# Neighbourhood attention in an encoder kernel: the value product as out[query, dim] in full tiles, the softmax division at the eviction, and q's low part padded with zeros

## The chip, the cores and the metric

The kernel runs on one core of one Trainium2 chip. The metric is device microseconds of that core from the start to the end of one execution, as the median of several runs. Five engines work side by side, each through its own list of instructions in order: PE (TensorE, matrix products), DVE (VectorE), ACT (ScalarE), POOL (GpSimd) and SP, which here only issues DMAs. [...]

## What is computed

One layer of a hybrid encoder over 16 meta tokens and 1024 tokens (a grid of 16 rows by 64 columns), width 1024. One input projection feeds three groups of heads, which are gated, concatenated and go through one output projection. The diff touches the first group, neighbourhood attention with 8 heads of 64, and in passing the second, gated linear attention (GLA) with 4 heads.

```python
s_loc = einsum('bhcd,bhrckd->bhcrk', qr, kw) * scale + bias      # a window of 8 rows x 16 columns of keys
s = concatenate([s_loc.reshape(B, H, GRID_W, wr * WIN_C), s_meta], axis=-1)
p = softmax(s, axis=-1)
o = einsum(p_loc, vw) + einsum(p_meta, vm_h)                     # then o * silu(g)
...
b = cumsum(g, axis=-2)                                           # GLA: within chunks of 64
```

## The kernel before

The program is built by a scheduler: Python generators emit instructions in an interleaved order, and the tile framework then orders each engine's list by its own timeline model, puts in the semaphores, and hands out the buffers of a tile's tag in rotation.

The work is staged. First comes the input projection (`proj_steps`, tile `pj`) interleaved with the RWKV branch, up to about 997 us. Then comes the stage that the change touches: for each pair of heads p = 0..3 the generator `na_mix(p)` is stepped by the loop at L1402, and at each step it is fed with five projection products of the next pair (`feed.pull`, tile `pj`), with one or two steps of GLA (`gla(h)`) and, for p = 3, with six products of the output projection (`out_pass`, tile `ops`). The output projection ends the program.

Float32 accuracy is kept by splitting: a tensor x is held as a rounded part and a remainder, both of type float32r (`whi`/`wlo`, `hhi`/`hlo`, `oh`/`ol`). For the scores, `na_k` stores per head e a tile `K[:, e]` whose one half of the partitions holds K and whose other half holds K's remainder; `na_q` stores q in `qA[:, e]` in both halves of the partitions and q's remainder in `qL`, where head e fills its own 64 partitions.

`na_mix(p)` goes over 16 items n: two halves of the query rows (hf), four column blocks (cb) and the two heads e of the pair, e innermost. One item is 128 queries (8 rows x 16 columns) against 288 to 416 keys:

- `score(n)` (L1194): two products into `sps`, q's high part (L1207, 128 rows) and its remainder (L1208, 64 rows). DVE adds the bias and takes the maximum into `sc` (L1211), ACT takes the exponent with the sum (L1216), DVE the reciprocal `rc` (L1218), and POOL multiplies `sc` by it and by 0.5 in place (L1219). `sc` has three buffers, `sps` one.
- `turn(n)` (L1223): three or four transposes of `sc` into `tps`, copied by ACT and DVE to `pT` (L1234).
- `value(n)` (L1241): for odd n, the products of both heads of the pair, `ops[half[e]]` with the values `VC` (or `VE` for the 17th row, 32 keys) as the stationary operand and `pT` moving. They write the transposed result out[dim, query] into tile `o_ps`, head 0 in partitions 0 to 63 and head 1 in 64 to 127. ACT copies it to `oT` (L1257). After the fourth column block POOL multiplies by the gate `gh` (L1259), and a DMA stores it (L1260).

The items overlap: at one step `score(n)`, `turn(n-1)` and `value(n-2)` are emitted.

In GLA (`gla(h)`, L1059) the head starts with a chain: `lps`, exponent and logarithm on ACT, a running sum over 17 chunks of 64 on DVE (three scans, L1080 to L1084, with the mask `smask`), two more exponents, the products `Q` and `MN`, then `aps`.

Of the kernel before, what the change touches and what calls it, by code (L numbers as in the profile page):

```python
# [12 lines left out]
ONB = 1  # L13
PM = 1
YM = 2
# [60 lines left out]
def emit(ctx, tc, a, out):  # L76
# [327 lines left out]
    def na_q(p, w):  # L404
        def ev_q(ps, n0, n1):
            third = (2 * p + n0 // 512) % 3 == 2
            pool = na if third else nst["pool"]
            qa = pool.tile([128, 2, 512], F32R, name="qA", bufs=1 if third else 2)
            ql = pool.tile([128, 512], F32R, name="qL", bufs=1 if third else 2)
            nst[p, "q", n0 // 512] = qa, ql  # L410
            blocked = lambda t: t.rearrange("p (b r c) -> p b r c", r=8, c=16)
            pv = ps.rearrange("p (r b c) -> p b r c", b=4, c=16)
            for e in range(2):
                S.copy(blocked(qa[half[e], e]), pv[half[e]])
            for e in range(2):
                V.tensor_tensor(out=blocked(ql[half[e]]), in0=pv[half[e]], in1=blocked(qa[half[e], e].bitcast(F32)), op=ALU.subtract)
                V.tensor_copy(qa[half[1 - e], e], qa[half[e], e].bitcast(F32))

        yield from proj_steps(w, GRID, ev_q)
# [629 lines left out]
    gl = gx.enter_context(tc.tile_pool(name="gl", bufs=1, side="right"))  # L1049
    smask = gl.tile([128, LP], BF16, name="smask2")  # L1050
    G.memset(smask, 1.0)
# [7 lines left out]
    def gla(h):  # L1059
# [9 lines left out]
        for (n0, n1) in FULL:  # L1069
# [9 lines left out]
        V.tensor_tensor(out=GB[:, PAD:], in0=MN[:, PAD:], in1=LG[:, PAD:], op=ALU.subtract)  # L1079
        V.tensor_tensor_scan(out=GB[0:64], data0=smask[0:64], data1=GB[0:64], initial=0.0, op0=ALU.mult, op1=ALU.add)  # L1080
        V.tensor_tensor_scan(out=GB[64:128, 0:C], data0=smask[64:128, 0:C], data1=GB[64:128, 0:C], initial=0.0,
                             op0=ALU.mult, op1=ALU.add)
        gr = GB[64:128, C:][:, ::-1]
        V.tensor_tensor_scan(out=gr, data0=smask[64:128, 0:T], data1=gr, initial=0.0, op0=ALU.mult, op1=ALU.add)  # L1084
        E1 = LG
# [41 lines left out]
        for n0 in range(0, NCH, 4):  # L1127
            m = min(4, NCH - n0)
            kps = pm.tile([64, 4, 128], F32, name="kps", tag="gt", bufs=2)
            for j in range(m):  # L1130
                PE.transpose(out=kps[:, j, :], in_=KD[:, (n0 + j) * C:(n0 + j + 1) * C], identity=ident)
            kdT = gl.tile([64, 4, 128], F32, name="kdT")
            S.copy(kdT[:, 0:m, :], kps[:, 0:m, :])
# [23 lines left out]
        for t0 in (0, 4):  # L1157
# [7 lines left out]
            ss = gl.tile([128, 4], F32, name="gs", bufs=2)  # L1165
            On = gl.tile([128, 4, 128], F32, name="On", bufs=ONB)
            for t in range(4):
# [15 lines left out]

    BT, SB, PTB = 3, 3, 2
    NE = G if 1 else V
    PTM = 1

    def na_mix(p):
        K, VC, VE = nst[p, "k"], nst[p, "v"], nst[p, "ve"]
        ohs = {}  # L1190
        order = [(hf, cb, e) for hf in range(2) for cb in range(4) for e in range(2)]
        us, bias = {}, {}

        def score(n):  # L1194
# [12 lines left out]
            PE.matmul(sv, lhsT=qa[:, e, cs], rhs=kv, start=True, stop=False)  # L1207
            PE.matmul(sv, lhsT=ql[es, cs], rhs=kv[es], start=False, stop=True)  # L1208
            sc = na.tile([128, 416], F32, name="sc", bufs=SB)
# [8 lines left out]
            V.reciprocal(rc, sm)  # L1218
            NE.tensor_scalar(out=sc[:, 0:m], in0=sc[:, 0:m], scalar1=rc, scalar2=0.5, op0=ALU.mult, op1=ALU.mult)  # L1219
            blocks = [(b, w, VC[0:w, cb, j, es] if j < 4 else VE[:, cb - 1, es]) for j, b, w in win_blocks(hf, cb)]  # L1220
            us[n] = sc, blocks

        def turn(n):  # L1223
            sc, blocks = us[n]
            tps = pm.tile([128, 4, 128], F32, name="tps", tag="t")
# [10 lines left out]
            else:  # L1236
                for j, (b, m, _) in enumerate(blocks):
                    (S.copy if j % 2 else V.tensor_copy)(pT[0:m, j, :], tps[0:m, j, :])
            us[n] = pT, blocks

        def value(n):  # L1241
            hf, cb, e = order[n]
            if not e:
                return
            pair = us.pop(n - 1), us.pop(n)
            ops = pm.tile([128, 128], F32, name="o_ps", tag="o")
            nb = len(pair[0][1])
            for j in range(nb):
                for e, (pT, blocks) in enumerate(pair):
                    _, m, vv = blocks[j]  # L1250
                    PE.matmul(ops[half[e]], lhsT=vv, rhs=pT[0:m, j, :], start=(j == 0), stop=(j == nb - 1))
            if hf not in ohs:
                gh = na.tile([128, 512], F32, name="gh")
                nc.sync.dma_start(out=gh, in_=nag[p][:, 512 * hf:512 * hf + 512])
                ohs[hf] = na.tile([128, 512], F32, name="oT"), gh
            oT, gh = ohs[hf]
            S.copy(oT.rearrange("p (r c) -> p r c", c=64)[:, :, 16 * cb:16 * cb + 16], ops.rearrange("p (r c) -> p r c", c=16))  # L1257
            if cb == 3:
                G.tensor_tensor(out=gh, in0=gh, in1=oT, op=ALU.mult)  # L1259
                nc.sync.dma_start(out=oscr[p][:, 512 * hf:512 * hf + 512], in_=gh)  # L1260

        TL, VL = 1, 2
        for n in range(16 + VL):
# [6 lines left out]
            if 0 <= n - VL < 16:  # L1270
                value(n - VL)
                if YM >= 3:
                    yield

# [282 lines left out]
```

## Time and profile before

| | us |
|---|---|
| median of three timed runs | 1490.52 (1487.98 to 1501.66) |
| the profiled execution | 1485.04 |
| its span, first to last instruction | 1482.8 |
| TensorE busy in the span | 1375.4 (93%) |
| DVE, ACT, POOL busy in the span | 886.2, 611.5, 665.7 |
| mean granted TensorE clock | 0.959 of full speed |

A matmul shows as a weight load (PEld) and a product (PE). A row of the timeline gives the start, how long it lasted, the engine, the line, out<-in by tile names, the array's tile shape (rows*columns of the stationary operand), the moving shape and how many followed each other. All products have the line of a helper (L93, transposes L96), so they are told apart by tiles. Products are pipelined: what one takes of the engine is the step from its start to the next start, and its recorded duration overlaps the next one's.

### The profile page before, as it was taken

To read this page: it belongs to the slowest core of one execution; us is meant where nothing else is said; L and a number is where in the kernel's file an instruction comes from. 1 tells how busy PE (TensorE), PEld (TensorE's weight loads), DVE (VectorE), ACT (ScalarE), POOL (GpSimd) and SP (SyncE) were. 2 spreads that over 40 slices of the span, in tenths; PEclk is the share of its full clock that TensorE was granted. 3 is DMA by queue.
4 is the path that set the end of the run, shared out by engine and by line. 5 is a ranking of instruction groups with operands and counts; after the bars stand their busy time and mean duration, and the time that the engine had idled before them with its cause. 6 is when DMAs were issued, how large, how long until landed. Compare 5 with 4: busy or idle time off the path is not lost. (4 is left out here: it accounts for less than half of the span.)

```text
span 1482.8 us, 36124 instructions
## 1 busy us (share of the span) xinstructions
PE 1375.4 (93%) x14656; PEld 1132.4 (76%) x14656; DVE 886.2 (60%) x1936; ACT 611.5 (41%) x1368; POOL 665.7 (45%) x775
## 2 busy tenths in 40 slices
PE   5888988999899999999999999998999989899997
PEld 4877777877788788788888888776677767667786
DVE  7425465676856565746656564546757577775554
ACT  5324243334443443434334332435465554644333
POOL 6435364464646664657656563223323132321223
PEclk9999898999989999999999999999999999899999
DMA  7655533433433444334333433155353423731432
GB/s 205 162 134 134 133 95 86 123 91 71 117 95 88 113 89 121 86 91 113 87 106 80 100 99 78 44 115 134 84 120 87 112 73 96 240 111 55 132 93 93
DMA packets 184806, 158.88 MB, mean 107 GB/s; under 512 B 19152, under 2 KB 168048, under 8 KB 184640
## 3 DMA queue, kind: packets, MB, share of 16 engines
q1 hardware_dynamic: 119616, 117.12, 26.6%
q0 software_dynamic: 63264, 35.20, 13.2%
q10 hardware_dynamic: 1760, 4.26, 0.8%
q8 instruction: 115, 1.88, 0.5%
q14 instruction: 51, 0.42, 0.1%
HBM read 123.81 MB, written 32.72 MB: 106 GB/s over the span
## 5 line engine op out<-in xcount | busy, mean ns | idle before, releaser
L93 PE MATMUL pj<-hhi,whi 128*128 128x348 f32 (+10 forms) x1088 | 378.9, 349 | 12.4 <-DVE zt L263 8.7
L93 PE MATMUL pj<-hlo,whi 128*128 128x348 f32 (+10 forms) x1088 | 377.0, 347 | 0.0
L93 PE MATMUL pj<-hhi,wlo 128*128 128x348 f32 (+8 forms) x1064 | 368.6, 347 | 1.7 <-POOL wlo L166 1.7
L93 PEld LDWEIGHTS pj<-hhi,whi 128*128 128x128 f32 (+1 forms) x1088 | 212.1, 195 | 28.2 <-issue 11.9
L93 PEld LDWEIGHTS pj<-hlo,whi 128*128 128x128 f32 (+1 forms) x1088 | 212.0, 195 | 12.9 <-issue 2.6
L93 PEld LDWEIGHTS pj<-hhi,wlo 128*128 128x128 f32 x1064 | 208.9, 196 | 14.4 <-issue 2.6
L166 POOL TENSOR_TENSOR wlo<-wraw,whi 128x512 fp32r<-128x512 f32 x94 | 125.6, 1337 | 144.6 <-DMA whi<-in_w_in_dram 53.6
L162 POOL DMA_DIRECT2D whi<-in_w_in_dram x94 | 74.7, 795 | 114.7 <-PE pj L93 101.3
L1219 POOL TENSOR_SCALAR sc<-sc,rc 128x288 f32<-128x288 f32 (+3 forms) x64 | 45.4, 710 | 163.9 <-DVE rc L1218 136.8
L845 POOL TENSOR_TENSOR dS<-SV,dec 64x128 f32<-64x128 f32 x128 | 59.1, 462 | 73.7 <-DVE SV L861 68.3
L699 POOL TENSOR_TENSOR BK<-BK,dec 64x1024 f32<-64x1024 f32 (+1 forms) x40 | 68.4, 1710 | 49.1 <-PE g L93 45.6
L791 ACT CAST XA<-ta 128x512 f16<-128x512 f32 (+1 forms) x92 | 49.9, 542 | 90.5 <-PE ta L93 87.3
L785 DVE TENSOR_TENSOR Fc<-fps,im 128x512 f16<-128x512 f32 (+1 forms) x92 | 58.5, 636 | 47.7 <-PE fps L93 43.6
L93 PE MATMUL ops<-hhi,oh 128*128 128x512 f32 x256 | 86.8, 403 | 0.0
L93 PE MATMUL g<-XR,BK 64*128 64x128 f32 (+1 forms) x544 | 67.6, 296 | 5.5 <-DVE GR L687 5.5
L93 PEld LDWEIGHTS g<-XR,BK 64*128 64x128 f32 x544 | 53.9, 192 | 16.5 <-issue 12.3
L1211 DVE CUSTOM_DVE_ANT_0 sc<-sps,bt 128x288 f32<-128x288 f32 (+3 forms) x64 | 33.3, 520 | 44.8 <-PE sps L93 30.4
L1328 DVE TENSOR_TENSOR yv<-ops,yv 128x512 f32<-128x512 f32 x48 | 33.0, 690 | 41.5 <-PE ops L93 41.3
L93 PEld LDWEIGHTS ops<-hhi,oh 128*128 128x128 f32 x256 | 48.6, 191 | 11.9 <-issue 1.0
L861 DVE TENSOR_TENSOR SV<-c,dS 64x128 f32<-64x128 f32 x128 | 36.7, 286 | 35.0 <-PE c L93 32.6
L257 ACT ACTIVATE zt<-pj,cols 128x347 f32<-128x347 f32 (+1 forms) x42 | 23.0, 549 | 82.5 <-PE pj L93 74.0
L93 PEld LDWEIGHTS <-Nh 64*64 64x64 f16 x1600 | 43.4, 111 | 15.0 <-issue 12.8
(302 smaller groups left out, 3048.7 us busy)
## 6 DMA issues: line engine op xcount, KB each, us to landing
whi<-in_w_in_dram POOLq DMA_DIRECT2D x94, 256.0 KB, 4.0
wraw<-in_w_in_dram SPq DMA_DIRECT2D x94, 256.0 KB
lr<-rwl POOLq DMA_DIRECT2D x32, 256.0 KB, 3.5
rwz<-zt SPq DMA_DIRECT2D x12, 544.0 KB
orr<-oscr SPq DMA_DIRECT2D x96, 64.0 KB
wr<-in_w_out_dram SPq DMA_DIRECT2D x12, 512.0 KB
glz<-zt SPq DMA_DIRECT2D x8, 544.0 KB
k<-rwz SPq DMA_DIRECT2D x32, 128.0 KB
```

The source lines that it names most:

```text
L93: return place(nc.tensor.matmul(*args, **kw))
L162: G.dma_start(out=hi, in_=w_v[:, q:q + 4, c0:c0 + 128])
L166: G.tensor_tensor(out=lo, in0=raw, in1=hi.bitcast(F32), op=ALU.subtract)
L257: S.activation(zt[:, PAD + n0:PAD + n1], ps[:, n0 - lo:n1 - lo], AF.Copy, scale=c1)
L699: G.tensor_tensor(out=bk, in0=bk, in1=dec[es, :, :, None, None].broadcast_to([64, 2, ns, 2, C]), op=ALU.mult)
L785: V.tensor_tensor(out=Fc, in0=fps, in1=mskt(l), op=ALU.mult)
L791: S.copy(A, aps)
L845: G.tensor_tensor(out=dS[es], in0=cur[es, :, e, :], in1=dcur[es, :, None].broadcast_to([64, 2, C]), op=ALU.mult)
L861: V.tensor_tensor(out=nx[es, :, e, :], in0=cps[es, 2], in1=dS[es], op=ALU.add)
L1211: V.tensor_tensor_reduce(out=sc[:, 0:m], in0=sps[:, 0:m], in1=bias[e][:, 0:m], scale=1.0, scalar=-3.0e38, op0=ALU.add, op1=ALU.max, accum_ ...
L1219: NE.tensor_scalar(out=sc[:, 0:m], in0=sc[:, 0:m], scalar1=rc, scalar2=0.5, op0=ALU.mult, op1=ALU.mult)
L1328: V.tensor_tensor(out=o, in0=ps, in1=o, op=ALU.add)
```

## The change

The value product is turned round. For each head e its own products are issued, `pT` as the stationary operand (128 queries) and the values moving (64 columns), into `o_ps[:, e]` as out[query, dim]; both heads of a pair share one PSUM tile. Since the queries are now on partitions, the division by the sum of exponents becomes the `scale` of the eviction on ACT (`AF.Copy` with `rc`), and the scaling on POOL goes. When a half's four column blocks are done, `close` transposes the four tiles [query, e and dim] into one PSUM tile `oT` (tag of `tps`, one buffer), DVE multiplies by 0.5 and the gate, and the DMA stores it.

q's remainder `qL` becomes two full tiles, one a head, with zeros in the other half of the partitions (a POOL memset each), so that both score products use 128 rows.

`sc` has two buffers instead of three, `smask` covers nine chunks instead of 17 (and the running sums are made in five scans instead of three), and `kdT` and `On` of GLA share a buffer.

```diff
-            ql = pool.tile([128, 512], F32R, name="qL", bufs=1 if third else 2)
+            ql = pool.tile([128, 2, 512], F32R, name="qL", bufs=1 if third else 2)
...
             for e in range(2):
-                V.tensor_tensor(out=blocked(ql[half[e]]), in0=pv[half[e]], in1=blocked(qa[half[e], e].bitcast(F32)), op=ALU.subtract)
+                G.memset(ql[half[1 - e], e].bitcast(F32), 0.0)
+                V.tensor_tensor(out=blocked(ql[half[e], e]), in0=pv[half[e]], in1=blocked(qa[half[e], e].bitcast(F32)), op=ALU.subtract)
...
-    smask = gl.tile([128, LP], BF16, name="smask2")
+    smask = gl.tile([128, 9 * C], BF16, name="smask2")
...
-        V.tensor_tensor_scan(out=GB[0:64], data0=smask[0:64], data1=GB[0:64], initial=0.0, op0=ALU.mult, op1=ALU.add)
-        V.tensor_tensor_scan(out=GB[64:128, 0:C], data0=smask[64:128, 0:C], data1=GB[64:128, 0:C], initial=0.0,
-                             op0=ALU.mult, op1=ALU.add)
-        gr = GB[64:128, C:][:, ::-1]
-        V.tensor_tensor_scan(out=gr, data0=smask[64:128, 0:T], data1=gr, initial=0.0, op0=ALU.mult, op1=ALU.add)
+        for hs, c0, c1, step in ((half[0], 0, 9, 1), (half[0], 9, 17, 1), (half[1], 0, 1, 1), (half[1], 9, 17, -1), (half[1], 1, 9, -1)):
+            gv = GB[hs, c0 * C:c1 * C][:, ::step]
+            V.tensor_tensor_scan(out=gv, data0=smask[hs, 0:(c1 - c0) * C], data1=gv, initial=0.0, op0=ALU.mult, op1=ALU.add)
...
-            kdT = gl.tile([64, 4, 128], F32, name="kdT")
+            kdT = gl.tile([64, 4, 128], F32, name="kdT", tag="kdT")
...
-            On = gl.tile([128, 4, 128], F32, name="On", bufs=ONB)
+            On = gl.tile([128, 4, 128], F32, name="On", tag="kdT")
...
-    BT, SB, PTB = 3, 3, 2
+    BT, SB, PTB = 3, 2, 2
...
-            PE.matmul(sv, lhsT=ql[es, cs], rhs=kv[es], start=False, stop=True)
+            PE.matmul(sv, lhsT=ql[:, e, cs], rhs=kv, start=False, stop=True)
...
-            NE.tensor_scalar(out=sc[:, 0:m], in0=sc[:, 0:m], scalar1=rc, scalar2=0.5, op0=ALU.mult, op1=ALU.mult)
...
         def value(n):
             hf, cb, e = order[n]
+            pT, blocks, rc = us.pop(n)
             if not e:
-                return
-            pair = us.pop(n - 1), us.pop(n)
-            ops = pm.tile([128, 128], F32, name="o_ps", tag="o")
-            nb = len(pair[0][1])
-            for j in range(nb):
-                for e, (pT, blocks) in enumerate(pair):
-                    _, m, vv = blocks[j]
-                    PE.matmul(ops[half[e]], lhsT=vv, rhs=pT[0:m, j, :], start=(j == 0), stop=(j == nb - 1))
+                acc[0] = pm.tile([128, 2, 64], F32, name="o_ps", tag="o")
+            ops, nb = acc[0][:, e], len(blocks)
+            for j, (_, m, vv) in enumerate(blocks):
+                PE.matmul(ops, lhsT=pT[0:m, j, :], rhs=vv, start=(j == 0), stop=(j == nb - 1))
...
-            oT, gh = ohs[hf]
-            S.copy(oT.rearrange("p (r c) -> p r c", c=64)[:, :, 16 * cb:16 * cb + 16], ops.rearrange("p (r c) -> p r c", c=16))
-            if cb == 3:
-                G.tensor_tensor(out=gh, in0=gh, in1=oT, op=ALU.mult)
-                nc.sync.dma_start(out=oscr[p][:, 512 * hf:512 * hf + 512], in_=gh)
+            oq, gh = ohs[hf]
+            S.activation(oq[:, cb, e], ops, AF.Copy, scale=rc)
+
+        def close(hf):
+            oq, gh = ohs[hf]
+            ot = pm.tile([128, 512], F32, name="oT", tag="t")
+            for cb in range(4):
+                PE.transpose(out=ot.rearrange("p (r b c) -> p r b c", b=4, c=16)[:, :, cb, :], in_=oq[:, cb].rearrange("p e d -> p (e d)"),
+                             identity=ident)
+            V.scalar_tensor_tensor(out=gh, in0=ot, scalar=0.5, in1=gh, op0=ALU.mult, op1=ALU.mult)
+            nc.sync.dma_start(out=oscr[p][:, 512 * hf:512 * hf + 512], in_=gh)
```

How the lists move. TensorE's list of the kernel before, early in the stage (first head pair, projection `pj` of the next pair's values, `vps` and `aps` of the first GLA head; a row is line, operation, out<-in, shape of the output and how many follow each other):

```order
L93 MATMUL pj<-hhi,whi 128x448
L93 MATMUL o_ps<-pT,VC 64x128 x4
L96 MATMUL vps<-ident,vT 128x128 x8
L93 MATMUL sps<-K,qA 128x384
L93 MATMUL sps<-K,qL 128x384
L96 MATMUL tps<-ident,sc 128x128 x3
L93 MATMUL o_ps<-pT,VC 64x128
L93 MATMUL pj<-hlo,whi 128x448
```

And the same place of the changed kernel:

```order
L93 MATMUL pj<-hhi,whi 128x448
L96 MATMUL tps<-ident,sc 128x128 x3
L93 MATMUL o_ps<-VC,pT 128x64
L93 MATMUL pj<-hlo,whi 128x448
L93 MATMUL pj<-hhi,wlo 128x448
L93 MATMUL sps<-K,qA 128x384
L93 MATMUL sps<-K,qL 128x384
L93 MATMUL pj<-hhi,whi 128x448
```

The value products of a pair stood as four of one run and one apart, each writing 64 partitions; now each head's stand by themselves, with all 128 partitions and 64 columns. The scores stand at other distances from them.

POOL's list of the kernel before, where the third pair's weights (`whi`, `wlo`) are loaded:

```order
L1219 TENSOR_SCALAR sc<-sc,rc 128x312 x2
L1219 TENSOR_SCALAR sc<-sc,rc 128x416
L1259 TENSOR_TENSOR gh<-gh,oT 128x512
L1219 TENSOR_SCALAR sc<-sc,rc 128x416
L162 DMA whi<-in_w_in_dram 128x4x128
L166 TENSOR_TENSOR wlo<-wraw,whi 128x512
```

And of the changed kernel:

```order
L479 COPY vW<-mt 128x24
L162 DMA whi<-in_w_in_dram 128x4x128
L166 TENSOR_TENSOR wlo<-wraw,whi 128x512
L416 MEMSET qL 64x512 x2
L162 DMA whi<-in_w_in_dram 128x4x128
L166 TENSOR_TENSOR wlo<-wraw,whi 128x512
```

The scalings and the gate products are gone from POOL, and two memsets per half stand between the weight loads.

TensorE's list of the changed kernel where the first pair's second half ends and a next pair's values are projected (`lps` starts the second GLA head):

```order
L93 MATMUL sps<-K,qA 128x288
L93 MATMUL sps<-K,qL 128x288
L96 MATMUL oT<-ident,oq 128x8x16 x3
L93 MATMUL pj<-hhi,whi 128x272
L93 MATMUL pj<-hlo,whi 128x272
L93 MATMUL lps<-gdT,gw 128x346
```

The four transposes of a half are new rows; before, nothing stood on TensorE between the last value product of a half and the next pair.

## Rows read from the trace of the kernel before

**Rows 1.** Stretches: us, busy us (x instructions) by engine, PEclk, DMA share, GB/s.
```profile
997.00:1392.00 395.00, 373.26 (x2446) 276.89 (x2444) 264.73 (x691) 204.08 (x499) 115.78 (x127) 0.97 0.42 116
```

**Rows 2.** Waits of TensorE, 997 to 1392 us: us in total, times, longest.
```profile
PE o_ps L93 <- DVE pT L1234: 6.5, 1, 6.5
PE vps L96 <- DMA vT<-glz: 4.8, 2, 3.3
PE tps L96 <- POOL sc L1219: 3.2, 3, 1.5
PE aps L93 <- DVE MN L1094: 2.5, 3, 1.3
```

**Rows 3.** Timeline of TensorE, one score pair: start us, us, what.
```profile
1034.81 0.29 PE L93 MATMUL sps<-K,qA 128*128 128x288 f32 x1
1035.03 0.40 PE L93 MATMUL sps<-K,qL 64*128 64x288 f32 x1
1035.35 0.41 PE L93 MATMUL pj<-hhi,wlo 128*128 128x320 f32 x1
1035.60 0.31 PE L93 MATMUL pj<-hhi,whi 128*128 128x320 f32 x1
1035.75 0.31 PE L93 MATMUL pj<-hlo,whi 128*128 128x320 f32 x1
```

**Rows 4.** Timeline of TensorE, two runs of value products.
```profile
1062.82 0.40 PE L93 MATMUL pj<-hhi,whi 128*128 128x512 f32 x1
1063.14 0.66 PE L93 MATMUL o_ps<-pT,VC 96*64 96x128 f32 x8
1063.73 0.50 PE L93 MATMUL pj<-hlo,whi 128*128 128x512 f32 x1
1064.07 0.40 PE L93 MATMUL pj<-hhi,wlo 128*128 128x512 f32 x1
1064.30 0.39 PE L93 MATMUL pj<-hhi,whi 128*128 128x512 f32 x1
...
1065.06 0.43 PE L93 MATMUL o_ps<-pT,VC 120*64 120x128 f32 x2
1065.42 0.50 PE L93 MATMUL pj<-hlo,whi 128*128 128x512 f32 x1
```

**Rows 5.** Groups by line: count, busy us, mean ns, idle us before, and what ended it.
```profile
L93 PE MATMUL o_ps<-pT,VC 128*64 128x128 f32 (+2 forms) x384 | 47.5, 294 | 6.7 <-DVE pT L1234 6.5 <-ACT pT L1234 0.2
L93 PE MATMUL o_ps<-pT,VE 32*64 32x128 f32 x32 | 6.8, 293 | 0.0
```

**Rows 6.** Timeline of TensorE at 72 us, full tiles with 64 moving columns.
```profile
72.41 0.27 PE L93 MATMUL lo<-lr,llo 128*128 128x64 f32 x1
...
73.08 0.28 PE L93 MATMUL lo<-lr,llo 128*128 128x64 f32 x1
```

**Rows 7.** Timeline of TensorE, eight transposes.
```profile
1114.93 1.09 PE L96 MATMUL vps<-ident,vT 128*128 128x128 f32 x8
1115.78 0.43 PE L93 MATMUL sps<-K,qA 128*128 128x384 f32 x1
```

**Rows 8.** Groups by line on POOL, DVE and ACT.
```profile
L1219 POOL TENSOR_SCALAR sc<-sc,rc 128x288 f32<-128x288 f32 (+3 forms) x64 | 45.4, 710 | 163.9 <-DVE rc L1218 136.8 <-DVE nm L1214 21.1 <-PE sps L93 4.7
L1259 POOL TENSOR_TENSOR gh<-gh,oT 128x512 f32<-128x512 f32 x8 | 10.3, 1283 | 12.2 <-ACT oT L1257 11.9
L572 POOL MEMSET llo<- 64x512 f32 x4 | 2.1, 520 | 0.2
L1177 DVE SCALAR_TENSOR_TENSOR gh<-ot,hc,gh 128x512 f32<-128x512 f32 x8 | 6.0, 748 | 2.0 <-PE ot L96 1.8
L1257 ACT COPY oT<-o_ps 128x128 f32<-128x128 f32 x32 | 8.5, 267 | 5.1 <-PE o_ps L93 5.1
```

**Rows 9.** The scans of a GLA head: ns min/median/max, first and last start.
```profile
L1080 DVE TENSOR_TENSOR_SCAN GB<-smask,GB x4: 2396/2414/4248, 1013.8 to 1279.6; 64x1088 f32<-64x1088 bf16 x4
L1081 DVE TENSOR_TENSOR_SCAN GB<-smask,GB x4: 287/364/2272, 1016.2 to 1283.9; 64x64 f32<-64x64 bf16 x4
```

More of the change, by code (lines that the diff above doesn't have):

```diff
@@ L1181, in gla @@
             yield
-    BT, SB, PTB = 3, 3, 2
-    NE = G if 1 else V
+    BT, SB, PTB = 3, 2, 2
     PTM = 1
@@ L1191, in na_mix @@
         order = [(hf, cb, e) for hf in range(2) for cb in range(4) for e in range(2)]
-        us, bias = {}, {}
+        us, bias, acc = {}, {}, [None]
         def score(n):
@@ L1218, in score @@
             V.reciprocal(rc, sm)
-            NE.tensor_scalar(out=sc[:, 0:m], in0=sc[:, 0:m], scalar1=rc, scalar2=0.5, op0=ALU.mult, op1=ALU.mult)
             blocks = [(b, w, VC[0:w, cb, j, es] if j < 4 else VE[:, cb - 1, es]) for j, b, w in win_blocks(hf, cb)]
-            us[n] = sc, blocks
+            us[n] = sc, blocks, rc
         def turn(n):
-            sc, blocks = us[n]
+            sc, blocks, rc = us[n]
             tps = pm.tile([128, 4, 128], F32, name="tps", tag="t")
@@ L1238, in turn @@
                     (S.copy if j % 2 else V.tensor_copy)(pT[0:m, j, :], tps[0:m, j, :])
-            us[n] = pT, blocks
+            us[n] = pT, blocks, rc
         def value(n):
             hf, cb, e = order[n]
+            pT, blocks, rc = us.pop(n)
             if not e:
-                return
-            pair = us.pop(n - 1), us.pop(n)
-            ops = pm.tile([128, 128], F32, name="o_ps", tag="o")
-            nb = len(pair[0][1])
-            for j in range(nb):
-                for e, (pT, blocks) in enumerate(pair):
-                    _, m, vv = blocks[j]
-                    PE.matmul(ops[half[e]], lhsT=vv, rhs=pT[0:m, j, :], start=(j == 0), stop=(j == nb - 1))
+                acc[0] = pm.tile([128, 2, 64], F32, name="o_ps", tag="o")
+            ops, nb = acc[0][:, e], len(blocks)
+            for j, (_, m, vv) in enumerate(blocks):
+                PE.matmul(ops, lhsT=pT[0:m, j, :], rhs=vv, start=(j == 0), stop=(j == nb - 1))
             if hf not in ohs:
@@ L1254, in value @@
                 nc.sync.dma_start(out=gh, in_=nag[p][:, 512 * hf:512 * hf + 512])
-                ohs[hf] = na.tile([128, 512], F32, name="oT"), gh
-            oT, gh = ohs[hf]
-            S.copy(oT.rearrange("p (r c) -> p r c", c=64)[:, :, 16 * cb:16 * cb + 16], ops.rearrange("p (r c) -> p r c", c=16))
-            if cb == 3:
-                G.tensor_tensor(out=gh, in0=gh, in1=oT, op=ALU.mult)
-                nc.sync.dma_start(out=oscr[p][:, 512 * hf:512 * hf + 512], in_=gh)
+                ohs[hf] = na.tile([128, 4, 2, 64], F32, name="oq"), gh
+            oq, gh = ohs[hf]
[8 more added lines that the diff above has]
+            nc.sync.dma_start(out=oscr[p][:, 512 * hf:512 * hf + 512], in_=gh)
         TL, VL = 1, 2
@@ L1271, in na_mix @@
                 value(n - VL)
-                if YM >= 3:
-                    yield
+            if n - VL == 8:
+                close(0)
+        close(1)
+        yield
     def piece(name, dt=F32R):
```

## The prediction, made before the changed kernel ran

> **What bounds the kernel now.** I read the stage first. The diff touches what runs from the first score product to the last value product, 997 to 1392 us. There TensorE is busy for 373.3 of 395.0 us, DVE for 264.7, ACT for 204.1, POOL for 115.8, at a granted clock of 0.97 [rows 1]. So the stage is as long as TensorE's own list of instructions, plus 21.7 us in which it waits. The waits, read next, stand at a few places: 6.5 us once for DVE's copies of pT, 4.8 us for a DMA, 3.2 us for the scaling on POOL, 2.5 us for DVE in a GLA head [rows 2]. A microsecond off TensorE's list is therefore a microsecond off the stage, as long as these waits don't grow; what moves between POOL, ACT and DVE costs nothing unless it lands in one of them. Before 997 us TensorE's order is the same row for row, and the last 91 us are the output projection, which the diff leaves alone.
>
> **What an instruction really takes.** Busy times of matmuls overlap, so I go by the step from one start to the next in the timeline. Full-tile products (128*128) follow each other at the pace of their columns: 320 columns step by 0.15 us [rows 3], 512 by 0.23 [rows 4]. At a change of tile shape the step grows. The score pair at 1034.81 shows it: the 128*128 high product of 288 columns steps by 0.22 to its 64*128 low product, which steps by 0.32 to the next pj, and that pj by 0.25 to the one behind it, instead of 0.15 [rows 3]. A full-tile run of the same three would take about 0.13 + 0.13 + 0.15 = 0.41 (288 columns as 288/320 of 0.147). The shape change costs 0.09 on the way in, and on the way out 0.19 plus 0.10 on the next product: 0.38 us a pair.
>
> **q's low part in full tiles.** There are 64 such pairs. In the order of before, 53 of the low products are followed by a full-tile instruction and lose all 0.38; 11 are followed by another small-tile one (seven times o_ps), where only the way in and the low product's own 0.10 go. 53 x 0.38 + 11 x 0.19 = 22.2; less 1 because some followers are transposes, whose step grows less: **-21 us**. K's columns streamed are the same; the longer contraction adds no column.
>
> **The value product turned round.** 208 f32 products are 416 recorded passes, two each, 384 with VC and 32 with VE [rows 5]. Now: 64 weight columns, 128 moving, heads e=0 and e=1 in the two column halves. Busy is 47.5 + 6.8 = 54.3 us [rows 5], but each stretch is counted about 0.07 past the start of what follows (eight passes: 0.66 busy, next start after 0.59 [rows 4]; two passes: 0.43 and 0.36 [rows 4]). The order of before has 93 runs of them, seven of which change from VC to VE inside, so 100 stretches: 54.3 - 100 x 0.07 = 47.3 us. Going in from a full tile costs 0.09 (pj at 1062.82 steps by 0.32, not 0.23), 72 times: 6.5. After a run the next full-tile instruction is late by 0.11 if a pj (1063.73 to 1064.07 [rows 4]), by about 0.04 if a transpose; at 0.07 for 87 exits: 6.1. Together 59.9 us.
> Afterwards: 128 weight columns, 64 moving, all in full tiles but the 16 products on VE, whose 32 rows remain a small tile. The trace of before has that shape once, in f32r: a row of 128*128 128x64 passes of which six steps take 0.67 us, from 72.41 to 73.08 [rows 6]: 0.112 each, 384 x 0.112 = 43.0. A VE product keeps its 0.36, gains about 0.05 for twice the weight columns, and keeps way in and out (0.16): 16 x 0.57 = 9.1. Sum 52.1, so **-8 us**.
> The unknown is the price of that pass in f32. Below: if its load lay wholly behind other work, the 64 columns would take half of what 128 moving f32 columns take, 0.053 (vps: eight in 0.85 us [rows 7]), and the kernel would gain another 384 x 0.059 = 23. Above: no overlap at all, which I bound by the 0.18 a pass that runs of two pay today, way out included [rows 4]: a loss of 384 x 0.068 = 26. I take 0.112, the row of the same shape.
>
> [...]
>
> **The four transposes per half.** 8 halves x 4 = 32 transposes at 0.107 each [rows 7]: **+3.5 us**, with no shape change.
>
> **Off TensorE.** POOL loses 64 scalings (45.4 us) and eight gate products of about 1.28 (10.3) and gains 16 memsets of 0.52 (8.3) [rows 8]. DVE gains eight products from PSUM at about 0.75 (6 us; the GLA gate of that shape takes 0.75 [rows 8]). ACT evicts 64 times 64 columns instead of 32 times 128 at 0.27; between 0.2 and 0.4 each that is 4 to 17 us more. All three lie beside TensorE, with at least 130 us free in the stage; if that cover went, the 6 us on DVE would show first, as DVE is the fullest. The chain from score to transpose loses the reciprocal and the scaling; of the 3.2 us that TensorE waits for it I credit 1, since the exponent is then the last to end. The GLA scan in five pieces instead of three: 0.29 for 64 and 2.40 for 1088 columns [rows 9] make 2.06 ns a column and 0.155 fixed, so 2 x 0.155 = 0.3 us per head, on a chain that TensorE does wait for (aps <- DVE MN [rows 2]): +1.2 for four heads.
>
> **Waits that are added.** With two sc buffers, the reduction of score n+2 on DVE waits for the transposes of score n on TensorE; behind it on DVE stand the evictions of pj, for which TensorE waits. o_ps of a pair holds its one bank over two steps, and the next pair's first product waits for the second eviction on ACT. oT shares its bank with tps, so one tps per half waits for DVE's gate product. The memset on POOL waits for the last score on the old buffer, and weight loads (whi) are issued behind it. The order puts pj or out-projection products between nearly all of these; I cost them at nothing, and at their full price below.
>
> **Sum.** -21 - 8 + 3.5 - 1 + 1.2 = -25.3. The profiled execution took 1485.04 (span 1482.8 and 2.2 around it): 1459.7. The median of the three timed runs is 5.5 above it, 1490.52, so the median to expect is **1465 us**.
>
> **Rivals.**
> *Given back.* The GLA heads hang on fixed chains (DMA of vT, scans, exponents) during which TensorE works off what the scheduler put beside them. With 25 us less to do it reaches these chains earlier and waits. For it: 7.3 of the 21.7 us are such waits of vps and aps [rows 2]. Against: they are four places only. If half comes back: 1478.
> *The column halves were worth more than I count.* The two heads ran side by side, and turned round they follow each other. If the 208 pairs of passes took 0.107 each as two that fully overlap, before was 22.3 and not 47.3, and the turn loses 25: 1490, no change. Against: eight passes take 0.59, but 56 of the 93 runs are a single product at 0.36. A load that nothing hides gives much the same, 1491. [...]
> *The score chain becomes the bound (slower).* One mechanism: the second sc buffer. If each of the 64 reductions holds DVE until transposes deep in TensorE's list, and TensorE then stands for evictions of pj, 0.8 us a score make 51: 1516. It eats the gain from 0.4 us a score. For it: DVE is the fullest helper. Against: the order leaves microseconds of pj between a score and its transposes, and the waits of today hold no row of 2 us or more for a reduction.
> *The load hides.* Pass at 0.053: 1442.
>
> **Chances.** Forecast 0.61 (own range 1455 to 1476), given back 0.18, column halves or load 0.10, score chain 0.06, load hides 0.05. About 1% (15 us) is what a measurement here can tell from no change. Faster by more: 0.61 and 0.05, and under half of "given back": 0.74. Within: the rest of it and the column case, 0.20. Slower: 0.06. The range runs from 1448 to 1486, leaving out the slower chain, the worst of the load and the full gain of a hidden one.
>
> **What would show it.** Right: sps low products with 128 rows stepping at 0.13 to 0.19 as the high ones do; o_ps 128*128 128x64 at 0.11 a step; steps of 0.22 to 0.34 around them gone except at VE, GLA and lps; TensorE's idle time in the stage near 22 us; the stage near 370. Wrong: o_ps steps of 0.16 or more; TensorE idle over 35 us, with DVE sc or pj evictions as what it waits for; DVE's reductions waiting for tps.

## The result, and the profile after

| | before | after |
|---|---|---|
| median of 20 timed runs each, us | 1489.97 (1483.46 to 1503.41) | 1478.62 (1475.10 to 1486.56) |
| ratio of the runs | | 0.9928, 95% interval 0.9909 to 0.9947 |
| profiled execution, its span | 1485.04, 1482.8 | 1480.26, 1478.5 |
| TensorE busy, DVE, ACT, POOL | 1375.4, 886.2, 611.5, 665.7 | 1356.0, 893.9, 619.0, 616.0 |
| granted clock over the span | 0.959 | 0.956 |

The change brings 11.4 us where I forecast 25. The direction held, and so did the wide range, which had the rivals in it; the time lies outside the forecast's own 1455 to 1476 and landed on the rival *given back* (1478). The profiled execution of before lies 4.9 us under its median and that of after 1.6 above, so the two traces differ by 4.8 us only; the medians carry the verdict, the traces the places. Of the kernels below, two had one execution each at about 1980 us and a granted clock of 0.55 to 0.56; these stand in no median or interval here.

The stage of after, in the columns of [rows 1]:

```profile
997.00:1392.00 395.00, 360.70 (x2496) 309.67 (x2496) 273.78 (x711) 212.71 (x532) 63.58 (x66) 0.95 0.42 118
```

In the same 395 us TensorE is busy for 360.7 instead of 373.3 us, and idle for 34.3 instead of 21.7. What it waits for, beside [rows 2]:

```profile
PE vps L96 <- DVE Vs L1111: 8.2, 3, 4.3
PE o_ps L93 <- DVE pT L1231: 6.8, 1, 6.8
PE vps L96 <- DMA vT<-glz: 3.6, 1, 3.6
PE tps L96 <- ACT sc L1214: 2.8, 3, 1.6
PE aps L93 <- DVE MN L1093: 2.5, 2, 1.3
```

The wait for POOL is gone, but 2.8 us for ACT's exponent stand in its place. The wait for copies of Vs grew most: in before it was one row that [rows 2] leaves out:

```profile
PE vps L96 <- DVE Vs L1112: 2.4, 1, 2.4
```

A list that got shorter and waits that grew can be told apart over the whole span: busy time times granted clock is an estimate of the list at full clock (in after, pj products of 272 columns step by 0.13 us at a clock of 1.00, at 1184 us, and by 0.23 at 0.50, at 1192 us). It was 1375.4 x 0.959 = 1319.0 and is 1356.0 x 0.956 = 1296.3. So the list lost 22.7 us, idle time over the span grew by 15.1 (1482.8 - 1375.4 = 107.4, now 122.5), and the time that low clock adds to the list grew by 3.3 in the same estimate: together the -4.3 us between the two spans.

The list itself, at its new steps (timeline of TensorE in the third GLA head):

```profile
1182.06 0.30 PE L93 MATMUL sps<-K,qA 128*128 128x288 f32 x1
1182.20 0.78 PE L93 MATMUL o_ps<-VC,pT 96*128 96x64 f32 x6
1182.79 0.38 PE L93 MATMUL sps<-K,qL 128*128 128x288 f32 x1
1183.00 0.28 PE L93 MATMUL pj<-hhi,whi 128*128 128x272 f32 x1
...
1184.92 0.29 PE L93 MATMUL pj<-hhi,wlo 128*128 128x272 f32 x1
1189.50 1.53 PE L96 MATMUL vps<-ident,vT 128*128 128x128 f32 x8 [4.29 <-DVE Vs L1111]
```

Six passes of a value product take 1182.79 - 1182.20 = 0.59, 0.10 each (0.11 in the median of the stage). The low product is a full tile and steps by 0.21 to the next pj, which steps by 0.12 to the one behind it; [rows 3] have 0.32 and 0.25. In the medians over the stage the low products step by 0.13 (288 columns) to 0.19 (416), as forecast; the high products still step by 0.21 to 0.28, so not all the longer steps around them are gone. Then TensorE stands for 4.29 us. What DVE does meanwhile, and ACT:

```profile
1181.33 1.24 DVE L1080 TENSOR_TENSOR GB<-MN,LG 128x1040 f32<-128x1040 f32 x1 [2.09 <-ACT LG L1078]
1182.68 6.04 DVE L1083 TENSOR_TENSOR_SCAN GB<-smask,GB 64x576 f32<-64x576 bf16 x5
1188.75 1.30 DVE L1111 COPY Vs<-vps 64x512 f32<-64x512 f32 x2
```
```profile
1183.24 0.31 ACT L1251 ACTIVATE oq<-o_ps,rc 128x64 f32<-128x64 f32 x1
1188.82 1.28 ACT L1086 ACT_TABLE_LOAD   x1 [5.26 <-DVE GB L1083]
```

The five scans of the head hold DVE for 6.0 us in one piece. The copies of Vs, of pT and the reductions are queued behind them; ACT has nothing to do for 5.3 us, and TensorE has worked off what lay ready. The same place of the program comes 6.6 us later in before, so I count 20 us from the subtraction that stands ahead of the scans (GB<-MN,LG). By engine, before:

```profile
1187.93:1207.93 20.00, 15.65 (x104) 12.09 (x101) 18.29 (x34) 10.45 (x24) 9.49 (x6) 0.83 0.39 110
```

and after:

```profile
1181.33:1201.33 20.00, 13.70 (x96) 12.12 (x96) 18.61 (x34) 8.96 (x20) 4.19 (x3) 0.74 0.46 120
```

DVE is busy for 18.6 of 20 us there, where over the whole stage it is for 273.8 of 395. It was for 18.3 before the change as well; what fell is TensorE's busy time beside it, from 15.7 to 13.7 us. The granted clock is at 0.74 in the mean of these 20 us (before 0.83): in both, part of the stretch behind the wait is run at a granted clock of 0.50, 1190.5 to 1200 us in after and 1197 to 1203 in before.

### The profile page after: what moved, and what is told of

The parts are those of the page before. It is cut to its first block, busy times and chain, and to the rows that moved or that the text cites. A ratio compares the mean times of both kernels' runs of the same rounds, so it can differ in the third digit from the quotient of the medians.

```text
span 1478.5 us, 36082 instructions
## 1 busy us (share of the span) xinstructions
PE 1356.0 (92%) x14688; PEld 1160.2 (78%) x14688; DVE 893.9 (60%) x1952; ACT 619.0 (42%) x1400; POOL 616.0 (42%) x719
## 5 line engine op out<-in xcount | busy, mean ns | idle before, releaser
L93 PEld LDWEIGHTS g<-XR,BK 64*128 64x128 f32 x544 | 53.7, 190 | 16.7 <-issue 12.5
L93 PEld LDWEIGHTS o_ps<-VC,pT 128*128 128x128 f32 (+2 forms) x384 | 53.5, 195 | 14.2 <-DVE pT L1231 7.2
L93 PE MATMUL o_ps<-VC,pT 128*128 128x64 f32 (+2 forms) x384 | 56.8, 272 | 8.0 <-DVE pT L1231 6.8
L862 DVE TENSOR_TENSOR SV<-c,dS 64x128 f32<-64x128 f32 x128 | 36.6, 286 | 34.8 <-PE c L93 32.5
L1214 ACT ACTIVATE sc<-sc,nm 128x288 f32<-128x288 f32 (+3 forms) x64 | 37.7, 588 | 45.5 <-DVE nm L1212 45.1
```

The source lines that it names most:

```text
L93: return place(nc.tensor.matmul(*args, **kw))
L862: V.tensor_tensor(out=nx[es, :, e, :], in0=cps[es, 2], in1=dS[es], op=ALU.add)
L1214: S.activation(sc[:, 0:m], sc[:, 0:m], AF.Exp, bias=nm, accum_out=sm)
```

## The experiments

One table holds what was measured; the ratio is to the kernel before, timed beside it on the same chip. Idle is 395 us less TensorE's busy time from 997 to 1392 us; the two kernels without GLA heads end the stage about 100 us earlier, and for them it is the idle time from the first score product to the last value product (996.5 to 1303.5 and 1005.6 to 1289.9 us). List is the estimate above, over the span (the clock's third digit makes it uncertain by 0.7, and kernels with the list of before scatter from 1315 to 1324).

| run | median us | ratio (95%) | idle | list |
|---|---|---|---|---|
| before | | | 21.7 | 1319 |
| after | 1478.6 | 0.9928 (0.9909 to 0.9947) | 34.3 | 1296 |
| pad alone (idle and list of the second run) | 1483.1, again 1479.8 | 0.9934 (0.9905 to 0.9963), 0.9928 (0.9901 to 0.9955) | 34.2 | 1299 |
| turn alone | 1484.4 | 0.9946 (0.9924 to 0.9968) | 19.9 | 1314 |
| room alone | 1494.6 | 1.0021 (0.9999 to 1.0044) | 27.9 | 1321 |
| before, no scans | 1477.5 | 0.9908 (0.9872 to 0.9944) | 12.6 | 1324 |
| after, no scans | 1452.6 | 0.9744 (0.9711 to 0.9777) | 19.0 | 1301 |
| before, no GLA heads | 1395.2 | 0.9361 (0.9323 to 0.9399) | 7.2 | 1247 |
| after, no GLA heads | 1378.1 | 0.9239 (0.9202 to 0.9277) | 15.9 | 1221 |
| after, scans beside | 1486.3 | 0.9968 (0.9943 to 0.9993) | 34.8 | 1295 |
| after, wait on POOL | 1478.6 | 0.9917 (0.9886 to 0.9948) | 38.6 | 1293 |
| after, scans woven | 1478.5 | 0.9925 (0.9900 to 0.9951) | 34.0 | 1297 |
| after, chain ahead | 1485.3 | 0.9960 (0.9932 to 0.9988) | 39.0 | 1297 |
| before, chain ahead | 1519.1 | 1.0208 (1.0168 to 1.0248) | 30.4 | 1315 |
| before, Vs on ACT | 1480.7 | 0.9945 (0.9921 to 0.9970) | 21.3 | 1315 |
| after, Vs on ACT | 1473.3 | 0.9883 (0.9848 to 0.9918) | 30.5 | 1296 |
| before, copies on ACT | 1481.5 | 0.9943 (0.9914 to 0.9971) | 16.0 | 1315 |
| after, copies on ACT | 1467.4 | 0.9850 (0.9816 to 0.9883) | 27.0 | 1295 |
| the same, low parts on DVE | 1462.5 | 0.9822 (0.9785 to 0.9859) | 24.7 | 1298 |

**The parts alone.** The pad with its room, in the kernel before, timed twice:

```diff
+                G.memset(ql[half[1 - e], e].bitcast(F32), 0.0)
...
-            PE.matmul(sv, lhsT=ql[es, cs], rhs=kv[es], start=False, stop=True)
+            PE.matmul(sv, lhsT=ql[:, e, cs], rhs=kv, start=False, stop=True)
...
-    BT, SB, PTB = 3, 3, 2
+    BT, SB, PTB = 3, 2, 2
```

> The kernel before with q's low part padded, and with the room that the pad needs (two sc buffers, five scans, kdT and On shared); the value product, the scaling on POOL and the eviction stay. Theory, given back: TensorE's list in the stage gets shorter by the 21 us that I forecast (low products with 128 rows, steps of 0.13 to 0.19), but its idle time in the stage rises from 21.7 us to about 30, at the GLA heads, and the time falls by 8 to 13 us, to 1477 to 1482. Rival, the list alone counts: idle time stays at 22 us, the time falls by 20, to 1470. Rival, the pad was sized too high: the steps at the low product stay above 0.25, the time falls by under 6 us.

> The kernel with the pad alone once more, for a trace at full clock. As before: 1477 to 1484, steps at the low products of 0.13 to 0.19 us, TensorE's busy time in the stage about 20 us under the kernel before and its idle time at about 30 us if the gain comes back in waits, at 22 if it doesn't.

Its list is some 20 us shorter, my 21; its time falls by 7 (1483.1 against 1490.6) and 10 us (1479.84 against 1489.90). The rest stands in these waits first of all:

```profile
PE vps L96 <- DVE Vs L1111: 15.3, 3, 7.4
PE tps L96 <- POOL sc L1218: 4.7, 3, 1.8
PE o_ps L93 <- DVE pT L1233: 3.8, 1, 3.8
```

The pad with its room gives half of its term back, at copies queued on DVE. The other part, the turn with q and the room as before (the diff at the head of the document without its lines on ql, smask, the scans, kdT, On and SB):

> The kernel with the value product turned round, the division at the eviction and the four transposes a half, but with q's low part as before (64 rows) and with the room of before (three sc buffers, three scans, kdT and On apart). My terms: -8, +3.5 and -1, so -5.5 us, 1484.5, if the list alone counts. Theory, given back: about half, 1486 to 1489, with idle time in the stage at 23 to 27 us. Rival, the turn itself costs time (column halves were worth more than I counted): 1490 or above, with TensorE's list in the stage no shorter.

1484.4 against 1490.6: 6 us (interval 5 to 11 by the ratio), its term of 5.5 in full, with idle time no longer than before; its list comes out 5 us shorter, which is within the scatter. The two alone bring about 9 and 6 us (10 and 8 by the ratios), both together 11. And the room by itself:

> The kernel before with nothing but the room that the change makes: two sc buffers, the short smask with five scans, kdT and On in one buffer. My sum says +1.2 us: 1491. If the second sc buffer or the shared kdT/On holds TensorE, 1495 or more, with new waits for DVE sc or ACT kdT in the stage. If the room is what ate the gain, +10 us or more: 1500.

3 to 4 us, between 0 and 7 by the interval: more than my 1.2 if anything; whether it is 1495 or more stays open. But its trace has two waits that before hardly has:

```profile
PE vps L96 <- DVE Vs L1110: 14.6, 3, 7.1
DVE sc L1209 <- PE tps L96: 13.5, 9, 2.0
```

With two sc buffers DVE's reductions wait for the transposes (in before they never do), and TensorE waits for the copies of Vs as long as in the pad alone, although this list is no shorter. So the wait for Vs doesn't come from the shorter list alone; up to 7 of the 14 us that the forecast missed can be the room's.

**Does the rest come back at the heads?** The scans left out in both kernels (the `tensor_tensor_scan` lines go, nothing else):

> The kernel before without the running sums of the GLA heads (the scans are left out, the rest of the chain stays), so that DVE is free for 5 to 9 us more in each of four heads. Its waits at the heads are then short: the idle time in the stage falls from 21.7 to about 15 us and the time by 5 to 9, to 1481 to 1485. It stands here for the comparison with the changed kernel without the same scans.

> The changed kernel without the running sums of the GLA heads, as its partner. Theory, given back because DVE is held by the scans: it gains more than its partner does, 12 to 18 us, to 1461 to 1467, so that the change is worth 18 to 22 us where the scans are away. Rival, the terms of my sum are too large by half: it gains as much as its partner, and the change is worth 9 to 13 us as with them.

Before gains 14 us, more than I expected, after 26. Without the scans the change is worth 1477.5 - 1452.6 = 24.9 us (the two intervals, as the root of their squares, leave 17 to 32), with them 11. The terms of my sum hold as far as that interval goes; the scans take half of their effect. After keeps its two sc buffers in this pair, so the buffers alone don't eat the gain. Then without the GLA heads at all:

> The kernel before without the GLA heads: each head only loads its gate and stores it, all its products, exponents and scans are left out. What stays in the stage is neighbourhood attention, the projections and the output projection. Some 40 to 60 us shorter, 1430 to 1450, with idle time of TensorE in the stage under 10 us. It stands here for the comparison with its partner.

> The changed kernel without the GLA heads, as its partner. Theory, the gain comes back at the fixed chains of the GLA heads: here there is none, and the change is worth what TensorE's list got shorter, 20 to 27 us. Rival, the terms are too large: it is worth 9 to 14 us here too. Rival, the score chain with its second sc buffer eats it: under 9 us, with waits of sps or tps for DVE and ACT in the stage.

The heads cost more than I thought, 96 us instead of 40 to 60. The change is worth 17 us here (9 to 25), between the theory and its rival. The list is 25 us shorter here too, and the idle time in the stage grows from 7.2 to 15.9, which fits: 25 - 9 is about 17. TensorE now waits at other places, first of all these:

```profile
PE o_ps L93 <- ACT oq L1136: 5.8, 5, 4.4
PE pj L93 <- POOL wlo L166: 2.8, 1, 2.8
```

So a part comes back without any head: the shorter list catches up with evictions and weights as well. The first row is the wait of a pair's first product for the second eviction on ACT, which the prediction named and costed at nothing.

**DVE held, or the chain too long?** The scans make DVE busy and they make the head's chain longer. Two runs were to part these. In the first the scans write to a tile that nobody reads at that time, so the exponents don't wait for them:

```diff
-            V.tensor_tensor_scan(out=gv, data0=smask[hs, 0:(c1 - c0) * C], data1=gv, initial=0.0, op0=ALU.mult, op1=ALU.add)
+            V.tensor_tensor_scan(out=SPf[hs, c0 * C:c1 * C], data0=smask[hs, 0:(c1 - c0) * C], data1=gv, initial=0.0, op0=ALU.mult, op1=ALU.add)
```

> The changed kernel with the five scans of a GLA head writing into a tile that nothing reads at that time (the running sums don't reach the exponents, which take the gates themselves). DVE is held as long and at the same place as in the changed kernel; the head's chain is as short as without the scans. If the gain is given back because DVE is held: 1474 to 1479, like the changed kernel. If it is given back because the chain from lps to aps is too long: 1454 to 1459, like the changed kernel without scans.

1486.3: the whole 26 us are lost again, and 8 more than in after, which no side of the expectation has. TensorE's order is nearly that of after (the last head ends behind 180 of the 208 value products here, behind 183 in after). Its longest waits:

```profile
PE vps L96 <- DVE Vs L1113: 7.4, 4, 2.6
PE o_ps L93 <- ACT oq L1252: 5.8, 2, 4.3
PE aps L93 <- DVE MN L1095: 5.1, 2, 2.7
```

Sums that nothing takes cost as much as sums that the exponents take, so what costs here is the time for which the scans hold DVE. But the run doesn't part DVE from the chain as it was meant to, since the chain isn't as short as without scans: the products Q and MN, for which `aps` waits, are DVE's own and are queued behind the scans (`aps` waits for MN for 5.1 us here, 2.5 in after). The second head here, then without scans:

```profile
1093.01 1.24 DVE L1080 TENSOR_TENSOR GB<-MN,LG 128x1040 f32<-128x1040 f32 x1 [2.09 <-ACT LG L1078]
1094.36 6.03 DVE L1085 TENSOR_TENSOR_SCAN SP<-smask,GB 64x576 f32<-64x576 bf16 x5
1103.87 1.28 DVE L1095 TENSOR_TENSOR MN<-MN,K 128x1088 f32<-128x1088 f32 x1
```
```profile
1088.69 1.24 DVE L1080 TENSOR_TENSOR GB<-MN,LG 128x1040 f32<-128x1040 f32 x1 [2.22 <-ACT LG L1078]
1094.04 1.28 DVE L1090 TENSOR_TENSOR MN<-MN,K 128x1088 f32<-128x1088 f32 x1
```

From the start of the subtraction to the end of MN these are 12.1 and 6.6 us; over the four heads 12.1 to 13.7 here, 6.6 to 10.3 without scans, 12.5 to 20.2 in after. In the other run the chain waits and DVE is free (a `G.tensor_scalar` of GB with 1.0, four times in the place of the scans):

> The other half of the pair: the changed kernel with the scans left out and four multiplications by one on POOL in their place (two of 128x576, two of 128x512, an estimate of 1.2 to 1.4 us each by the 0.71 us of a 128x288 scaling on POOL), so that the head's chain is about 5 us longer and DVE is free. If DVE being held is the cause: 1454 to 1460. If the length of the chain is: 1472 to 1479.

1478.6, which contradicts DVE as the only cause, but this run doesn't decide: the framework, which orders the lists by its own timeline, moved the heads behind the scores. The value products end at 1346.8 us here, 20 us ahead of the last head's own end; in after they end at 1385.7 and lie beside it:

```profile
L93 PE MATMUL o_ps<-VC,pT x384: 217/275/421, 998.6 to 1346.8; 128*128 128x64 f32 x96, 96*128 96x64 f32 x80, 120*128 120x64 f32 x16
...
L96 PE MATMUL ot<-ident,On x32: 270/273/447, 1075.2 to 1367.1; 128*128 128x128 f32 x32
```

and much of its idle time stands there (17 us from 1320 on: `ops` for ACT oh 6.9, `ot` for On 6.6, `ops` for SP 3.8), while no `vps` waits for DVE any more. Two runs that change the order alone ended the same way. The first puts other work of DVE between the scans (a no-sync dependency of a scan on the copy or the negated maximum written before it), the second writes the next head's chain ahead:

> The changed kernel with the five scans of a GLA head taken apart: between two of them DVE's order has a copy of Vs, a copy of pT or a reduction of the scores, and the loads and transposes of vT are written ahead of the scans. The same arithmetic. Theory, given back at the heads because the scans hold DVE for 5 to 9 us in one piece: the waits of vps for Vs (8.2 us) and of o_ps for pT (6.8 us) shrink to under 5 together, the idle time in the stage falls from 35 to about 25 us, the time from 1478.6 to 1466 to 1472. Rival, it is the length of the head's chain and not the order on DVE: the waits move to aps, which then waits for the later exponents, and the time stays within 3 us of 1478.6 or rises.

> The changed kernel with the chain of the next GLA head (lps to the last exponent and dec) written ahead of the running states of the head before, and dec in two buffers. The same arithmetic; the scans still hold DVE for as long, but three of the four heads find their exponents done when they start. If the length of the chain is what gives the gain back, the lps to aps distance no longer matters and the time falls by 8 to 14 us, to 1465 to 1471, with idle time of TensorE in the stage at about 25 us. If DVE being held is the cause, the wait stands in another place and the time stays within 4 us of 1478.6.

> The kernel before with the same chain ahead. Its waits at the heads are smaller, so it has less to win: 3 to 8 us, 1482 to 1487. Given back at the heads says that the change is then worth 15 to 22 us; terms too large says 11.

Woven: no change. Here, too, the value products end early, at 1362.3 us. Ahead: 6.7 us slower in after, 28 slower in before, far from the 3 to 8 us that I expected it to win there. Both orders shift the waits to other places; neither is a way out.

**Take work out from behind the scans.** ACT stands idle while DVE scans, so the copies go there:

```diff
-                V.tensor_copy(Vs[64:128, n0 + 1:n0 + 1 + mu_, :], ps[64:128, 0:mu_, :])
+                S.copy(Vs[64:128, n0 + 1:n0 + 1 + mu_, :], ps[64:128, 0:mu_, :])
...
-                    (S.copy if (j2 - j == 2 if PTM == 1 else j % 2) else V.tensor_copy)(pT[0:m, j:j2, :], tps[0:m, j:j2, :])
+                    S.copy(pT[0:m, j:j2, :], tps[0:m, j:j2, :])
```

The first line alone, in after and in before:

> The changed kernel with both halves of the copies of Vs on ACT (the upper half was DVE's). ACT stands idle for 3 to 5 us at each head while DVE makes the scans. The same arithmetic, TensorE's list nearly the same. Theory, DVE is held by the scans and TensorE waits for what is queued behind them: the wait of vps for DVE Vs (8.2 us) goes, the scans start up to 0.7 us earlier, idle time in the stage falls from 36 to 25 to 29 us and the time by 5 to 10, to 1469 to 1474. Rival, TensorE waits at the next thing behind the scans just as long (the maximum, pT): within 3 us of 1478.6.

> The kernel before with the same copies on ACT. It waits for Vs for 2.4 us alone, so the theory gives 1 to 4 us, 1487 to 1490, and the change is then worth 14 to 20 us; the rival leaves the change at 11.

After gains 5 us, as expected; before gains 9, more than I gave it, so the change is worth 7 here (9 by the ratios, 3 to 16) where I expected 14 to 20. Both lines, in after and in before:

> As the run with Vs on ACT, and the remaining copies of pT (one block of 96 or 120 keys an item, 0.28 us) on ACT too, so that only the reductions of the scores and the head's own products are queued behind the scans. Theory: another 3 to 6 us, as the wait of o_ps for DVE pT (6.8 us) goes: 1464 to 1470. Rival, ACT becomes the bound (its busy time rises by 18 us in the stage): 1476 or more, with waits of o_ps for ACT pT.

> The kernel before with the copies of Vs and pT on ACT. With Vs alone it gained 8 us, more than its 2.4 us of waits for Vs. Theory: with less behind the scans the change is worth more than its 11 us: here 1478 to 1483, so 11 to 16 us against the changed kernel with the same copies (1467.4). If relief at the heads is worth the same to both kernels, so that it says nothing on the change: 1474 to 1476 and 7 to 9 us, as with Vs alone.

1467.4 and 1481.5. The second line takes 6 us more from after and nothing from before; the change is worth 14 us (7 to 21), which isn't clear of its 11 without these copies. The waits for Vs and pT of DVE are gone, what is left first of all is the reductions (`PE sps <- DVE mx`, 11.9 us, longest 7.0). The longest one lies in the fourth head, where the scans take not 5 but 9.2 us. This is DVE there, and POOL at the same time:

```profile
1266.04 9.25 DVE L1083 TENSOR_TENSOR_SCAN GB<-smask,GB 64x576 f32<-64x576 bf16 x5
```
```profile
1268.41 4.68 POOL L1294 TENSOR_TENSOR hhi<-wr,hhi 128x1024 fp32r<-128x1024 f32 x2 [48.21 <-ACT hhi L1293]
```

Last, these subtractions of the output weights go to DVE, behind the scans:

```diff
-            (G if op is None or (i + 0) % 2 else V).tensor_tensor(out=lo, in0=raw, in1=hi.bitcast(F32), op=ALU.subtract)
+            (G if op is not None and i % 2 else V).tensor_tensor(out=lo, in0=raw, in1=hi.bitcast(F32), op=ALU.subtract)
```

> The changed kernel with the copies of Vs and pT on ACT, and the low parts of the output weights (a subtraction of 128x1024, 2.5 us each on POOL) on DVE. The same arithmetic. In the changed kernel the scans of the fourth head take 8.9 us where those of the second take 5.0, and two such subtractions run on POOL beside them. If POOL holds the scans up: the fourth head's five scans take 5.0 to 5.3 us, TensorE's waits there shrink by some 3 us, and the time falls by 1 to 4 from 1467.4, less what the subtractions take of DVE (1.2 us each behind the scans). If something else does (the DMAs of that stretch): 8 to 9 us as before.

The same place in its trace:

```profile
1269.99 5.00 DVE L1083 TENSOR_TENSOR_SCAN GB<-smask,GB 64x576 f32<-64x576 bf16 x5
```

5.00 us, so POOL's subtractions held the scans up, and not the DMAs of that stretch. The time is 1462.5, which the interval doesn't part from 1467.4; the longest wait for a reduction falls to 3.3 us. It is the fastest kernel of this study that computes the whole layer: 1.8% under before, 1.1% under after.

## Why the prediction was wrong, step by step

*q's low part, -21.* The list of the pad alone is some 20 us shorter. Right in size, though the steps of the high products stayed longer than I said.

*The value product, -8, and the four transposes, +3.5.* Forecast together -4.5. The list of the turn alone says -5, within the scatter, its time -6 (5 to 11); the pass takes 0.10 to 0.11 (forecast 0.112). The 32 transposes are there. Right within what these can tell.

*Off TensorE.* Costs of single instructions, in groups of after:

```profile
L1251 ACT ACTIVATE oq<-o_ps,rc 128x64 f32<-128x64 f32 x64 | 20.0, 313 | 11.2 <-PE o_ps L93 8.8 <-PE oT L96 2.3
L416 POOL MEMSET qL<- 64x512 f32 x16 | 8.3, 519 | 22.3 <-PE sps L93 19.4 <-DMA nag<-zt 2.4
L1259 DVE SCALAR_TENSOR_TENSOR gh<-oT,gh 128x512 f32<-128x512 f32 x8 | 5.5, 685 | 0.1
L1083 DVE TENSOR_TENSOR_SCAN GB<-smask,GB 64x512 f32<-64x512 bf16 (+2 forms) x20 | 26.0, 1348 | 0.2
```

ACT pays 0.31 an eviction, inside my 0.2 to 0.4; memsets 8.3 as forecast; the gate product 0.69 (forecast 0.75). The scans take 26.0 us in 20 pieces. In before they take, in 12:

```profile
L1080 DVE TENSOR_TENSOR_SCAN GB<-smask,GB 64x1088 f32<-64x1088 bf16 x4 | 11.5, 2868 | 0.1
L1084 DVE TENSOR_TENSOR_SCAN GB<-smask,GB 64x1024 f32<-64x1024 bf16 x4 | 11.1, 2784 | 0.0
L1081 DVE TENSOR_TENSOR_SCAN GB<-smask,GB 64x64 f32<-64x64 bf16 x4 | 3.3, 822 | 0.1
```

25.9: the two pieces more cost 0.1 in all, not 1.2, though single pieces vary too much for that to be exact. The credit of 1 us for POOL's scaling came to 0.4 at most (3.2 us for POOL before, 2.8 for ACT after).

*The step that failed* is the one that turned the list into time: "A microsecond off TensorE's list is therefore a microsecond off the stage, as long as these waits don't grow." They grew, from 21.7 to 34.3 us. I did name the rival, but gave it 0.18, because "they are four places only". That counted the places at which TensorE waited already, not those at which it was about to; and it left out the 2.4 us for Vs, with which 9.7 and not 7.3 of the 21.7 us stood at the heads. The same holds for "with at least 130 us free in the stage" of the work off TensorE: DVE's free time is a mean over 395 us, while around the scans of a head it has little, and what TensorE gains on it ahead of them is lost behind them. This could be read from stretches of before, as at its first head, where DVE is busy for 18.97 of 20 us:

```profile
1010.00:1030.00 20.00, 18.69 (x141) 13.94 (x140) 18.97 (x38) 10.61 (x26) 9.41 (x10) 0.85 0.32 91
```

Counted from the subtraction ahead of the scans, DVE was busy for 18.6, 17.6, 18.3 and 19.7 of 20 us at the four heads of before, and for 16.4, 18.1, 18.6 and 19.7 in after. It was about as full there before the change; what fell is TensorE's busy time beside it, from 18.7, 17.2, 15.7 and 13.5 us to 13.7, 16.2, 13.7 and 11.3.

A second step failed with it, the waits that the change adds, which I costed "at nothing". DVE's reductions do wait for tps in after, one of my own signs of being wrong:

```profile
DVE sc L1209 <- PE tps L96: 8.1, 7, 2.4
```

What this costs in time by itself no run says; the room, which brings it, costs 3 to 4 us (0 to 7) where I had 1.2.

What I said would show the step right didn't come: idle time at 34 us and not near 22, and the stage, from the first score product at 995.6 to the last value product at 1385.7, took 390 us and not near 370.

*The rivals.* Column halves: the turn alone brings its term in full, so no. The score chain by the second sc buffer: the room alone adds 3 to 4 us, TensorE waits for reductions for 1.7 us in after, and without the scans the change is worth its 25 us with two buffers; so it isn't the bound, though a few us can be its. A load that hides (0.053 a pass) or that nothing hides (0.18, the bound taken from runs of two): passes at 0.10 to 0.11, so neither. No run shows the 0.16 a pass that my signs of being wrong name; in its place stand these 0.10 to 0.11.

*What is shown and what isn't.* Shown: the list got shorter by about what I forecast; without the scans the change is worth twice as much; scans whose sums nothing takes lose the gain as fully, so there it is the time for which they hold DVE; taking copies out from behind them brings 11 us in after, and 8 in before as well. Not settled: whether the scans cost by the copies and reductions queued behind them or by the head's own products, since no run kept the chain short with DVE held, and every run that changed the chain's length otherwise also changed the order; how much of the loss is the room's; whether the change is worth more with the copies on ACT; and why the kernel before gained 9 us from Vs on ACT although its trace showed 2.4 us of waits for it. A lead for the last: with Vs on ACT its four heads take 12.0 to 12.7 us from the subtraction to MN, where they took 13.5 to 21.0, the longest with POOL's subtractions beside its scans.

## What to carry to other kernels

When the list of the engine that bounds a stage is cut, read the free time of its helpers stretch by stretch, not over the stage: here half of the gain stopped where a helper holds its queue with one long run of instructions, and the waits that were to grow there were small in the trace of before. Compare stretches from the same instruction on, not from the same time. Then move the short instructions that the bounding engine waits for to an engine that stands idle during that run; the two changes of order tried here only moved the waits. Busy time times granted clock, an estimate of the list, tells beside idle time a list that didn't shrink from one that shrank for nothing (here 22.7 us less list, 15.1 us more idle time).

## What the runs showed of the hardware that was not expected

A run of five scans on DVE took 9.25 us with two subtractions on POOL beside it and 5.00 without. A product of 128x1088 in after took 3.43 us under a POOL subtraction that ran from 1289.85 to 1292.89, where the other heads' takes 1.28:

```profile
1290.61 3.43 DVE L1093 TENSOR_TENSOR MN<-MN,K 128x1088 f32<-128x1088 f32 x1
```
```profile
1289.85 3.04 POOL L1294 TENSOR_TENSOR hhi<-wr,hhi 128x1024 fp32r<-128x1024 f32 x1 [8.45 <-ACT hhi L1293]
```

The product ended 1.15 us after POOL's subtraction did (1294.04 and 1292.89), which is about the 1.28 that it takes at the other heads.

Work on DVE whose result nothing took, 23.1 us in four runs of scans, cost 34 us (1452.6 without, 1486.3 with it), in a stage in which DVE is free for 124 of 395 us.
